# Twenty-four pairs of chunks of a value pass, multiplied by seven products of halves

## The chip, the cores and the metric

The kernel runs on one core of a Trainium2 chip. The metric is the device time of one execution in microseconds, lower is better. The kernel before was timed three times: 1837.2, 1838.18 and 1838.45 us, median 1838.18. The engines are named as in the profile: PE is TensorE, PEld its weight loads, DVE is VectorE, ACT is ScalarE, POOL is GpSimd, SP is the engine whose queue issues the loads.

## The reference

A two-layer decoder trunk over 256 tokens of width 1024. Each layer has a token mixer (mLSTM in layer 0, RG-LRU in layer 1) beside a memory cross-attention, a layer norm, a mixture of 16384 experts of one hidden unit each, and a second layer norm. What matters here is the expert step, which picks 128 experts for every token (8 heads of 16):

```python
u = u_tab[eid]
act = jax.nn.gelu(jnp.einsum('nhkd,nd->nhk', u, xb))
coef = (gw * act)
return jnp.einsum('nhk,nhkd->nd', coef, v_tab[eid])
...
x = layer_norm(DN_ALPHA * x + y, ln2_g[i], ln2_b[i])
```

Everything is float32.

## The kernel before

The kernel doesn't gather the experts. It computes the activations of all 16384 experts for all 256 tokens, multiplies them by a weight that is zero for an expert that wasn't picked, and multiplies the result with the whole value table. So each layer has two long passes over tables of 64 MB: the u pass, which makes activations, and **the value pass**, which the change is about.

The value pass goes over 128 chunks of 128 experts, `for i in range(P)` from L1104 in `peer_layer`. Chunk i has a coefficient tile of 128 experts x 256 tokens (a block of `wglo` for i < 64, of `wghi` from there on) and a value tile of 128 experts x 1024 columns, loaded from HBM into `raw`. The output y is 256 x 1024, held in four PSUM banks of 128 tokens x 512 columns over the whole pass.

**Three products for one.** The products run on values rounded to a shorter form (fp32r). Each operand is split into a rounded part H and a remainder L, and `mm3` (L165 to L169) issues H x H, H x L and L x H. A chunk has 2 token halves x 2 column halves x 3 = 12 products of 128x128 by 128x512.

**Preparing a chunk.** `pump` (L77) splits a value tile: ACT casts `raw` to `wH` (L97), and DVE subtracts to get `wL` (L112); `pool_cols` is 0 in this pass, so POOL takes no part of it. Then it issues the next load on SP's queue (`load`, L117). `coef` (L1083) does the same for the coefficients through `split_to` (L221): ACT casts to `cH` (L222), DVE subtracts to get `cL` (L223).

**What sets the order.** The program is scheduled by hand: each engine executes its instructions in the order in which they are written. Iteration i first calls `self.next`, which splits the value tile of chunk i + 2, then `coef(i + 2)`, then issues the products of chunk i. `wH`/`wL` and `cH`/`cL` have three buffers each (`HL_BUFS`), `raw` has five; a load is issued while fewer than five raw tiles are in flight (`n_flight`), and a raw tile is let go when it has been split. So a cast to `wH` for chunk i + 2 must wait until PE is done with chunk i - 1.

**Beside the pass.** In layer 0 the loads for the next layer's cross-attention are put between the value chunks by `plan` (L1182 to L1190): four tiles of `memT` (split by ACT and POOL) and four of `wkv` (split by ACT and DVE into `kH`, `kL`). When i + 2 reaches `N0` = 64 the memory of `wglo` is given to them (L1108); in layer 1 it is given to three extra value tiles (`eH`, `eL`) for the pass's end. The last chunks of the pass (`kept`) are multiplied bank by bank, so that the layer norm can begin on one bank while PE is at the next. `norm` (L254) first adds each bank onto x, scaled by `ALPHA` (L272).

Of the kernel before, what the change touches and what calls it, by code (L numbers as in the profile page):

```python
# [7 lines left out]
F32 = mybir.dt.float32  # L8
F32R = mybir.dt.float32r
# [4 lines left out]
ALU = mybir.AluOpType  # L14
# [4 lines left out]
P = 128  # L19
D = 1024  # L20
T = 256
DT = 8
ALPHA = 4.0 ** 0.25
EPS = 1e-5
GSCALE = 32768.0
N0 = 64
# [7 lines left out]
EXTRA = 3  # L34
MIX_COLS = 0
GAP = 56
CAND = [(0, 1, 16, 0), (1, 1, 8, 16), (2, 1, 5, 24), (3, 1, 4, 29), (4, 1, 3, 33), (5, 3, 2, 36), (8, 8, 1, 42)]
NCAND = 50
ROWS = [(16, 16), (24, 8), (29, 5), (33, 4), (36, 3), (38, 2), (40, 2), (42, 2)]
# [5 lines left out]
class Trunk:  # L45
    def __init__(self, ctx, tc, A, out):
        self.ctx, self.tc, self.nc, self.A, self.out = ctx, tc, tc.nc, A, out
        pool = lambda name, bufs=1, **k: ctx.enter_context(tc.tile_pool(name=name, bufs=bufs, **k))
        self.const = pool("const")
        self.raw = pool("raw", RAW_BUFS)  # L50
        self.hl = pool("hl", HL_BUFS)
        self.small = pool("small", 2)
        self.ps = pool("ps", 8, space=PSUM)
        self.items = []
        self.flip = False
        self.sides = []
        self.n_load = self.n_split = self.n_got = self.n_flight = 0
        self.kept = {}
        self.loaded, self.split = {}, {}

    def bank(self):
# [15 lines left out]
    def pump(self, upto):  # L77
        nc = self.nc
        upto = min(upto, len(self.items))
        while self.n_split < upto:  # L80
            i = self.n_split
            self.load(i + 1)
            ap, n, dest, keep, cuts = self.items[i]
            r = self.loaded.pop(i)
            self.n_split += 1
            if keep is not None:
                self.kept[keep] = r
                continue
            if type(dest) is int:
                h, l = self.extra[dest]  # L90
            elif dest is None:
                h = self.hl.tile([P, D], F32R, name="wH")[:, :n]
                l = self.hl.tile([P, D], F32R, name="wL")[:, :n]
            else:
                h, l = dest()
            for c in cuts:
                (nc.vector.tensor_copy if self.cast_dve else nc.scalar.copy)(h[:, c], r[:, c])  # L97
            k = n if getattr(dest, "pool", False) else min(n, self.pool_cols)
            if len(cuts) > 1:
                for c in cuts:  # L100
                    e = (nc.vector, nc.gpsimd)[c.start > 0]
                    e.tensor_sub(l[:, c], r[:, c], h[:, c].bitcast(F32))
                k = n
            elif k and self.chained:
                nc.vector.tensor_sub(l[:, k:], r[:, k:], h[:, k:].bitcast(F32))  # L105
                k += 2
                nc.gpsimd.tensor_sub(l[:, :k], r[:, :k], h[:, :k].bitcast(F32))  # L107
                k = n
            elif k:
                nc.gpsimd.tensor_sub(l[:, :k], r[:, :k], h[:, :k].bitcast(F32))  # L110
            if k < n:
                nc.vector.tensor_sub(l[:, k:], r[:, k:], h[:, k:].bitcast(F32))  # L112
            self.split[i] = (h, l)
            self.n_flight -= getattr(dest, "stage", None) is None
            self.load(len(self.items))

    def load(self, upto):  # L117
# [135 lines left out]

    def norm(self, y, last, early, fill=False):  # L254
        nc, x = self.nc, self.x
        fine = early or last
        while "b" not in self.kept:
            self.pump(self.n_split + 1)
        g, b = self.kept["g"], self.kept["b"]
# [4 lines left out]
        Q = 256  # L264

        def add(tt, k):
            if fine and tt and k:
                q0, n = 1 + k, 1
            else:
                q0, n = 2 * k, 2  # L270
            xs = x[:, tt, q0 * Q:(q0 + n) * Q]
            nc.vector.scalar_tensor_tensor(xs, xs, ALPHA, y[tt][k][:, :n * Q], op0=ALU.mult, op1=ALU.add)  # L272
            return tt, q0, n

        def half(tt, q0, n):
# [71 lines left out]
        else:  # L347
            yield
            part = add(1, 0)
# [3 lines left out]
        if early:  # L353
            yield
            part = add(1, 0)
# [611 lines left out]
    def peer_layer(self, layer):  # L967
        nc, tc, A = self.nc, self.tc, self.A
        with ExitStack() as ctx:
# [4 lines left out]
            lo = right.enter_context(tc.tile_pool(name=f"lo{layer}", bufs=1, side="right")).tile([P, N0, T], F32,  # L974
                                                                                               name="wglo")
# [104 lines left out]
            self.pool_cols, self.chained = 0, False  # L1080
            kept = HL_BUFS + (EXTRA if layer else 0)

            def coef(i):  # L1083
                src = lo[:, i, :] if i < N0 else hi[:, i - N0, :]
                pool, z = (ends, i - P + kept) if layer and i >= P - kept else (cp, "")
                cH = pool.tile([P, T], F32R, name=f"cH{z}")
                cL = pool.tile([P, T], F32R, name=f"cL{z}")
                self.split_to(cH, cL, src)
                return cH, cL
            cs = [coef(0), coef(1)]  # L1090
            g = self.u_step()
            gl = cp.tile([P, T], F32, name="gl", bufs=1)
            nc.scalar.activation(gl, g, AF.Gelu)
            nc.vector.tensor_mul(hi[:, nj - 1, :], hi[:, nj - 1, :], gl)
            y = [[self.bank() for _ in range(2)] for _ in range(2)]
            late = []

            def products(tt, c0, n, part):
                t = slice(tt * P, (tt + 1) * P)
                k, o = divmod(c0, 512)  # L1100
                for i_, (h, l), (cH, cL) in part:
                    self.mm3(y[tt][k][:, o:o + n], cH[:, t], cL[:, t], h[:, c0:c0 + n], l[:, c0:c0 + n],
                             i_ == 0, i_ == P - 1)
            for i in range(P):  # L1104
                if i + 2 > P - 1:
                    self.pool_cols = 512
                late.append((i, self.next(min(HL_BUFS, P - i)), cs.pop(0)))
                if i + 2 == N0:  # L1108
                    right.close()
                    if layer == 0:  # L1110
                        kv = self.later.enter_context(tc.tile_pool(name="kv1", bufs=1, side="right"))
                        m = right.enter_context(tc.tile_pool(name="mem1", bufs=1, side="right"))
                        self.mem_dest(kv, m)
                        m.tile([P, 80], F32, name="gap")
                        self.kvw = [(m.tile([P, D], F32R, name=f"kH{c}"), m.tile([P, D], F32R, name=f"kL{c}"))
                                    for c in range(4)]
                    else:
                        ends = right.enter_context(tc.tile_pool(name="ends", bufs=1, side="right"))
                        self.extra = [(ends.tile([P, D], F32R, name=f"eH{e}"), ends.tile([P, D], F32R, name=f"eL{e}"))
                                      for e in range(EXTRA)]  # L1120
                if i + 2 < P:
                    cs.append(coef(i + 2))
                if i + 1 > P - kept:
                    continue
                for tt in range(2):
                    for k in range(2):
                        products(tt, 512 * k, 512, late)
                late = []
            self.pool_cols = MIX_COLS
            if layer:  # L1130
# [17 lines left out]
    def plan(self):  # L1148
# [24 lines left out]
        def tail(layer):  # L1173
            for i, dt in enumerate((6, 7, 0, 1, 2, 3, 4, 5)):
                self.add(A["w_out"][layer, dt], D, i - 2 if 0 <= i - 2 < EXTRA else None)
            norm("ln1", layer)
            for g in range(2):
                for dt in range(DT):
                    self.add(A["w_q"][layer, g, dt], D)
            for i in range(P):  # L1180
                self.add(A["u"][layer, i], D)
            for i in range(P):  # L1182
                e = i - P + HL_BUFS + EXTRA
                self.add(A["v"][layer, i], D, e if layer and 0 <= e < EXTRA else None)
                k = (i - N0 - 4) // 6
                if layer == 0 and i > N0 and (i - N0 - 4) % 6 == 0 and 0 <= k < 8:
# [106 lines left out]
```

## Time and profile before

The profiled execution of the kernel before:

| what | us |
|---|---|
| its own time | 1838.14 |
| its span | 1836.4 |
| layer 0's value pass, first product to last (start) | 581.5 to 929.5 |
| PE busy in the span | 1806.4 |
| PEld busy | 1665.8 |
| DVE busy | 1297.5 |
| ACT busy | 941.4 |
| POOL busy | 433.1 |

The time lies 1.7 us above the span: the span runs from the first to the last instruction of the profile. A row of the groups view has the line, engine and operation, the tiles written and read, the shape, the count, then the busy time, the mean duration of one in ns, and the idle time of the engine ahead of it with what ended it. A row of the timeline has start and duration in us; what stands in brackets is the engine's idle time before it and what ended that. Line numbers in these rows are those of the kernel before.

### The profile page before, as it was taken

The numbers are of one execution on the slowest core, as the hardware profiler recorded it, in microseconds if no ns is written. First come the engines' busy times: TensorE is split into PE (matmuls) and PEld (weight loads), VectorE is DVE, ScalarE is ACT, GpSimd is POOL, SyncE is SP. The second block draws the span as 40 slices with busy tenths as digits, with TensorE's granted clock in tenths as the row PEclk, the third lists the DMA queues.
The fourth block names the chain that finished last, engine by engine and source line by source line (L and its number), as shares of the span: only waits on it lengthen the run. The fifth ranks groups of instructions, "written<-read, shape, count | busy, mean of one in ns | idle before, by whom it ended". The sixth has DMA issues, their size and how long they took to land.

```text
span 1836.4 us, 33231 instructions
## 1 busy us (share of the span) xinstructions
PE 1806.4 (98%) x12756; PEld 1665.8 (91%) x12756; DVE 1297.5 (71%) x2652; ACT 941.4 (51%) x1608; POOL 433.1 (24%) x324
## 2 busy tenths in 40 slices
PE   8999999999999999999999899999999999999998
PEld 8999999999999888888898699999999988888886
DVE  5674669599998555666568648795999965555556
ACT  6554555455545444555547355554555455555443
POOL 2005772333331000000011368335333300000000
PEclk9999999999999999999999899999999999999999
DMA  6656566655555666667654355666555566666664
GB/s 235 208 158 187 173 186 194 195 172 162 161 161 164 192 196 193 195 217 226 209 186 133 118 174 183 192 196 187 161 162 161 162 182 194 193 192 193 194 194 137
DMA packets 95265, 334.21 MB, mean 182 GB/s; under 512 B 10621, under 2 KB 13697, under 8 KB 94849
## 3 DMA queue, kind: packets, MB, share of 16 engines
q1 hardware_dynamic: 93464, 328.93, 58.6%
q10 hardware_dynamic: 1640, 3.15, 0.5%
q8 instruction: 100, 1.64, 0.4%
q14 instruction: 61, 0.49, 0.1%
HBM read 330.98 MB, written 1.05 MB: 181 GB/s over the span
## 4 chain that ended last, share of the span: by engine, by line
PE 73%; issue 15%; POOL 7%; DVE 3%; ACT 2%; DMA 0%; POOLq 0%; DVEq 0%; SPq 0%; ACTq 0%
PE bank L167 23%; PE bank L169 23%; PE bank L168 23%; POOL wL L107 7%; PE bank L226 2%; ACT wH L97 1%; DVE wL L112 0%; PE bank L319 0%; DVE aa L765 0%; DVE xc L731 0%; POOL wL L110 0%; DVE st L278 0%; DVE x L272 0%; ACT pr L451 0%; DMA cp<-in_rg_par_dram 0%
## 5 line engine op out<-in xcount | busy, mean ns | idle before, releaser
L97 ACT CAST wH<-raw 128x1024 fp32r<-128x1024 f32 (+2 forms) x605 | 628.6, 1040 | 772.5 <-PE bank L169 323.3
L112 DVE TENSOR_TENSOR wL<-raw,wH 128x1024 fp32r<-128x1024 f32 (+3 forms) x410 | 464.1, 1134 | 452.1 <-ACT wH L97 451.4
L167 PE MATMUL bank<-xHL,wH 128*128 128x256 f32 x2536 | 717.5, 283 | 7.1 <-ACT wH L97 6.2
L169 PE MATMUL bank<-xHL,wL 128*128 128x256 f32 x2536 | 704.5, 278 | 2.2 <-DVE wL L112 2.2
L168 PE MATMUL bank<-xHL,wH 128*128 128x256 f32 x2536 | 704.6, 278 | 0.0
L167 PEld LDWEIGHTS bank<-xHL,wH 128*128 128x128 f32 x2536 | 479.5, 189 | 7.9 <-ACT wH L97 6.2
L169 PEld LDWEIGHTS bank<-xHL,wL 128*128 128x128 f32 x2536 | 479.3, 189 | 3.1 <-DVE wL L112 2.8
L168 PEld LDWEIGHTS bank<-xHL,wH 128*128 128x128 f32 x2536 | 479.9, 189 | 0.3 <-DVE xHL L223 0.3
L168 PE MATMUL bank<-wL,cH 128*128 128x512 f32 x1015 | 394.3, 388 | 0.0
L169 PE MATMUL bank<-wH,cL 128*128 128x512 f32 x1015 | 394.3, 388 | 0.0
L167 PE MATMUL bank<-wH,cH 128*128 128x512 f32 x1015 | 394.3, 388 | 0.0
L110 POOL TENSOR_TENSOR wL<-raw,wH 128x1024 fp32r<-128x1024 f32 (+1 forms) x121 | 259.1, 2145 | 212.8 <-ACT wH L97 212.2
L169 PEld LDWEIGHTS bank<-wH,cL 128*128 128x128 f32 x1015 | 190.5, 188 | 39.7
L167 PEld LDWEIGHTS bank<-wH,cH 128*128 128x128 f32 x1015 | 190.5, 188 | 39.4
L168 PEld LDWEIGHTS bank<-wL,cH 128*128 128x128 f32 x1015 | 190.5, 188 | 39.0
L107 POOL TENSOR_TENSOR wL<-raw,wH 128x386 fp32r<-128x386 f32 x126 | 129.6, 1029 | 280.0 <-DVE wL L105 280.0
L308 POOL TENSOR_TENSOR x<-x,raw 128x256 f32<-128x256 f32 x6 | 4.8, 805 | 556.7 <-ACT x L305 556.7
L929 DVE TENSOR_TENSOR oh<-iota,i12T 128x1024 f16<-128x1024 f16 x128 | 130.2, 1017 | 0.0
L105 DVE TENSOR_TENSOR wL<-raw,wH 128x640 fp32r<-128x640 f32 x126 | 103.9, 825 | 7.7
L932 DVE TENSOR_TENSOR oh<-oh,gT 128x1024 f16<-128x1024 f16 x128 | 90.0, 703 | 4.4
L1062 PE MATMUL bank<-oh 128*128 128x128 f16 x1024 | 80.9, 220 | 1.1 <-DVE oh L932 1.1
L1062 PEld LDWEIGHTS <-oh 128*128 128x128 f16 x1024 | 58.8, 97 | 6.0 <-DVE oh L932 1.5
(273 smaller groups left out, 1527.7 us busy)
## 6 DMA issues: line engine op xcount, KB each, us to landing
raw<-in_u_dram SPq DMA_DIRECT2D x256, 512.0 KB, 3.7
raw<-in_v_dram SPq DMA_DIRECT2D x256, 512.0 KB, 4.3
raw<-in_w_q_dram SPq DMA_DIRECT2D x32, 512.0 KB, 3.8
raw<-in_w_out_dram SPq DMA_DIRECT2D x16, 512.0 KB, 4.5
raw<-in_w0qx_dram SPq DMA_DIRECT2D x8, 512.0 KB, 4.8
raw<-in_wkv_dram SPq DMA_DIRECT2D x8, 512.0 KB, 4.7
raw<-in_w1x_dram SPq DMA_DIRECT2D x8, 512.0 KB, 4.5
raw<-in_w0v_dram SPq DMA_DIRECT2D x8, 384.0 KB, 6.1
```

What stands on the lines that cost most here:

```text
L97: (nc.vector.tensor_copy if self.cast_dve else nc.scalar.copy)(h[:, c], r[:, c])
L105: nc.vector.tensor_sub(l[:, k:], r[:, k:], h[:, k:].bitcast(F32))
L107: nc.gpsimd.tensor_sub(l[:, :k], r[:, :k], h[:, :k].bitcast(F32))
L110: nc.gpsimd.tensor_sub(l[:, :k], r[:, :k], h[:, :k].bitcast(F32))
L112: nc.vector.tensor_sub(l[:, k:], r[:, k:], h[:, k:].bitcast(F32))
L167: mm(out, sH, mH, start=start, stop=False, skip_group_check=True)
L168: mm(out, sH, mL, start=False, stop=False, skip_group_check=True)
L169: mm(out, sL, mH, start=False, stop=stop, skip_group_check=True)
L226: self.nc.tensor.matmul(out, lhsT, rhs, start=start, stop=stop, skip_group_check=True)
L929: nc.vector.tensor_tensor(flat(oh[:, 1:3]), self.iota2.unsqueeze(1).to_broadcast([P, 4, P, 2]), pairs(self.i12T[:, j]), op=ALU.is_equal)
L932: nc.vector.tensor_tensor(flat(oh[:, 0:2]), two.rearrange("p z (q e t) -> p z q e t", q=2, t=2), pairs(self.gT[:, j]), op=ALU.mult)
L1062: nc.tensor.matmul(wp[:, qs], oh[:, 2, q // 2, :, q % 2], oh[:, z, q // 2, :, q % 2], start=z == 0, stop=z == 1, skip_group_check=True)
```

## The change

In each value pass the chunks are seen in groups of eight, and in most groups (`PAIRS`: eleven in layer 0, thirteen in layer 1) the third and the fourth chunk, 8k + 2 and 8k + 3, are multiplied together as a 2 x 2 block product: two chunks by two halves of the tokens on one side, two chunks by two halves of the columns on the other. Strassen's scheme (in Winograd's form) needs seven block products in place of eight. Each is three products on PE as before.

The seven products are spread over the group. Chunk 8k + 2 has one (into the new bank `m1`), chunk 8k + 3 has two (into `y[0][0]` and `y[0][1]`). Three (`m5`, `m7`, `m6`) follow behind the products of chunk 8k + 7, and the last (`y[1][0]`) behind those of chunk 8k + 8. The four m banks are kept over the whole pass, and are combined once, behind the last pair, by `onto` and the additions on `q`; that scales x by `ALPHA` there, so `norm` doesn't.

The operands of the scheme are sums. DVE makes them in float32 in blocks of `wglo` or `wghi` whose chunks are done (`sums32`); then ACT casts them and DVE subtracts, as for any operand, into the tile `xHL`, which isn't used otherwise in this pass (`th`, `tl` for the value sums, `sh`, `sl` for the coefficient sums). `paired(i)` issues these steps at set places of the group, behind `coef(i + 2)` and ahead of the products of chunk i. The raw tiles of the pair are held until the step at 8k + 4 has read them. Of the first chunk of a pair only the first 512 columns are split.

The memory of `wglo` is given away later (`CLOSE` = 76 in place of 64), and layer 0's extra loads stand after every fifth chunk from 80 in place of every sixth from 68.

```diff
+PAIRS = [[1, 2, 3, 4, 5, 6, 7, 8, 9, 11, 12], list(range(1, 14))]
+CLOSE = 76
...
+            z = self.twin.get(i)
+            if z is not None:
+                self.pair[z] = r
+                n = min(n, 512 * (z + 1))
+                cuts = [slice(0, n)]
...
-            self.n_flight -= getattr(dest, "stage", None) is None
+            self.n_flight -= getattr(dest, "stage", None) is None and z is None
...
+            th, tl = self.xHL[:, 0:3, :], self.xHL[:, 3:6, :]
+            sh, sl = (self.xHL[:, f, :].rearrange("p (f t) -> p f t", f=4) for f in (6, 7))
...
+            def split_sums(k, f, n, s):
...
+                nc.vector.tensor_sub(tl[:, s:s + n], t, plain(th[:, s:s + n]))
+            def cast_sums(k, f, n, s):
...
+                nc.scalar.copy(th[:, s:s + n], t)
+            def paired(i):
+                k, j = divmod(i, 8)
+                if k - 1 in PAIRS[layer] and j == 0:
+                    cast_sums(k - 1, 3, 1, 0), split_sums(k - 1, 3, 1, 0)
+                if k in PAIRS[layer]:
+                    t, s = sums32(k)
+                    if j in (2, 4):
+                        (a0, a1), (b0, b1) = [[r[:, :512], r[:, 512:]] for r in self.pair]
+                    if j == 0:
+                        (ta, ua), (tb, ub) = part(i + 2), part(i + 3)
+                        nc.vector.tensor_sub(s[:, 1], ta, ua)
+                        nc.vector.tensor_sub(s[:, 2], ub, s[:, 1])
+                        nc.vector.tensor_add(s[:, 0], ua, ub)
+                        nc.scalar.copy(sh[:, 0:3], s[:, 0:3])
+                    elif j == 2:
+                        nc.vector.tensor_sub(t[0], a1, a0)
+                        nc.vector.tensor_sub(t[1], b1, a1)
+                        cast_sums(k, 0, 2, 0)
+                    elif j == 4:
+                        nc.vector.tensor_add(t[2], t[1], a0)
+                        nc.vector.tensor_sub(t[3], b0, t[2])
+                        cast_sums(k, 2, 1, 2)
+                        self.n_flight -= 2
+                        self.load(len(self.items))
+                    elif j == 5:
+                        split_sums(k, 0, 2, 0)
+                    elif j == 6:
+                        split_sums(k, 2, 1, 2)
...
             def coef(i):
...
+                if i in first:
+                    cH, cL = cp.tile([P, T], F32R, name="cH"), cp.tile([P, T], F32R, name="cL")
+                    self.split_to(cH[:, :P], cL[:, :P], src[:, :P])
+                    return cH, cL
+                if i - 1 in first:
...
+                    nc.vector.tensor_sub(s[:, 3], src[:, :P], s[:, 2])
+                    nc.scalar.copy(cH[:, :P], src[:, :P])
+                    nc.scalar.copy(cH[:, P:], s[:, 3])
+                    nc.scalar.copy(sh[:, 3], src[:, P:])
+                    nc.vector.tensor_sub(cL[:, :P], src[:, :P], plain(cH[:, :P]))
+                    nc.vector.tensor_sub(cL[:, P:], s[:, 3], plain(cH[:, P:]))
+                    nc.vector.tensor_sub(sl[:, 0:3], s[:, 0:3], plain(sh[:, 0:3]))
+                    nc.vector.tensor_sub(sl[:, 3], src[:, P:], plain(sh[:, 3]))
+                    return cH, cL
...
+            m1, m5, m7, m6 = [self.bank() for _ in range(4)]
...
                 if i + 2 < P:
                     cs.append(coef(i + 2))
+                paired(i)
...
+                if i in first or i - 1 in first:
+                    (_, (h, l), (cH, cL)), = late
+                    if i in first:
+                        mixed(m1, h[:, :512], l[:, :512], (cH[:, :P], cL[:, :P]), first[i])
+                    else:
+                        mixed(y[0][0], h[:, :512], l[:, :512], (cH[:, :P], cL[:, :P]))
+                        mixed(y[0][1], h[:, 512:], l[:, 512:], (cH[:, P:], cL[:, P:]))
+                else:
+                    for tt in range(2):
+                        for k in range(2):
+                            products(tt, 512 * k, 512, late)
+                if i % 8 == 7 and i // 8 in PAIRS[layer]:
+                    for f, b in enumerate((m5, m7, m6)):
+                        mixed(b, th[:, f], tl[:, f], (sh[:, f], sl[:, f]), i // 8)
+                if i % 8 == 0 and i // 8 - 1 in PAIRS[layer]:
+                    mixed(y[1][0], th[:, 0], tl[:, 0], (sh[:, 3], sl[:, 3]))
```

More of the change, by code (lines that the diff above doesn't have):

```diff
@@ L58, in __init__ @@
         self.kept = {}
+        self.twin, self.pair = {}, [None, None]
         self.loaded, self.split = {}, {}
@@ L111, in pump @@
             if k < n:
-                nc.vector.tensor_sub(l[:, k:], r[:, k:], h[:, k:].bitcast(F32))
+                nc.vector.tensor_sub(l[:, k:n], r[:, k:n], h[:, k:n].bitcast(F32))
             self.split[i] = (h, l)
-            self.n_flight -= getattr(dest, "stage", None) is None
+            self.n_flight -= getattr(dest, "stage", None) is None and z is None
             self.load(len(self.items))
@@ L255, in norm @@
         nc, x = self.nc, self.x
+        alpha = 1.0 if last or fill else ALPHA
         fine = early or last
@@ L271, in add @@
             xs = x[:, tt, q0 * Q:(q0 + n) * Q]
-            nc.vector.scalar_tensor_tensor(xs, xs, ALPHA, y[tt][k][:, :n * Q], op0=ALU.mult, op1=ALU.add)
+            nc.vector.scalar_tensor_tensor(xs, xs, alpha, y[tt][k][:, :n * Q], op0=ALU.mult, op1=ALU.add)
             return tt, q0, n
@@ L1081, in peer_layer @@
             kept = HL_BUFS + (EXTRA if layer else 0)
-            def coef(i):
-                src = lo[:, i, :] if i < N0 else hi[:, i - N0, :]
+            block = lambda i: lo[:, i, :] if i < N0 else hi[:, i - N0, :]
+            part = lambda i: [block(i)[:, :P], block(i)[:, P:]]
+            first = {8 * k + 2: k for k in PAIRS[layer]}
+            done = 8 * PAIRS[layer][-1] + 8
+            gl = cp.tile([P, T], F32, name="gl", bufs=1)
+            th, tl = self.xHL[:, 0:3, :], self.xHL[:, 3:6, :]
@@ new lines, in peer_layer, with sums32 @@
+            sh, sl = (self.xHL[:, f, :].rearrange("p (f t) -> p f t", f=4) for f in (6, 7))
+            plain = lambda a: a.bitcast(F32)
+            def sums32(k):
+                old = hi if k > 8 else lo
+                flat = lambda b: old[:, b:b + 2, :].rearrange("p a b -> p (a b)")
+                return [flat(b) for b in (0, 2, 4, 6)], flat(8).rearrange("p (f t) -> p f t", f=4)
+            def split_sums(k, f, n, s):
+                old = hi if k > 8 else lo
+                t = old[:, 2 * f:2 * (f + n), :].rearrange("p (f a) b -> p f (a b)", f=n)
+                nc.vector.tensor_sub(tl[:, s:s + n], t, plain(th[:, s:s + n]))
@@ new lines, in cast_sums, with onto @@
+            def cast_sums(k, f, n, s):
+                old = hi if k > 8 else lo
+                t = old[:, 2 * f:2 * (f + n), :].rearrange("p (f a) b -> p f (a b)", f=n)
+                nc.scalar.copy(th[:, s:s + n], t)
[27 more added lines that the diff above has]
+                        split_sums(k, 2, 1, 2)
+                q = hi[:, 0:2, :].rearrange("p a b -> p (a b)")
+                def onto(t, h, src, scale=ALPHA):
+                    xs = self.x[:, t, 512 * h:512 * h + 512]
+                    nc.vector.scalar_tensor_tensor(xs, xs, scale, src, op0=ALU.mult, op1=ALU.add)
+                n = i - done
+                if n == 1:
+                    nc.scalar.copy(q, m1)
+                    onto(0, 0, m1)
+                elif n == 2:
+                    nc.vector.tensor_add(q, q, m6)
+                elif n == 3:
+                    onto(0, 1, q)
+                elif n == 4:
+                    onto(0, 1, m5, 1.0)
+                elif n == 5:
+                    nc.vector.tensor_add(q, q, m7)
+                elif n == 6:
+                    onto(1, 0, q)
+                elif n == 7:
+                    onto(1, 1, q)
+                elif n == 8:
+                    onto(1, 1, m5, 1.0)
@@ new lines, in mixed @@
+            def mixed(out, mh, ml, stat, k=None):
+                self.mm3(out, *stat, mh, ml, k == PAIRS[layer][0], k == PAIRS[layer][-1])
+            def coef(i):
+                src = block(i)
+                if i in first:
[3 more added lines that the diff above has]
+                if i - 1 in first:
+                    cH, cL = cp.tile([P, T], F32R, name="cH"), cp.tile([P, T], F32R, name="cL")
+                    _, s = sums32(i // 8)
+                    nc.vector.tensor_sub(s[:, 3], src[:, :P], s[:, 2])
[7 more added lines that the diff above has]
+                    return cH, cL
@@ L1091, in peer_layer @@
             g = self.u_step()
-            gl = cp.tile([P, T], F32, name="gl", bufs=1)
             nc.scalar.activation(gl, g, AF.Gelu)
@@ L1107, in peer_layer @@
                 late.append((i, self.next(min(HL_BUFS, P - i)), cs.pop(0)))
-                if i + 2 == N0:
+                if i + 2 == CLOSE:
                     right.close()
@@ L1122, in peer_layer @@
                     cs.append(coef(i + 2))
+                paired(i)
                 if i + 1 > P - kept:
                     continue
-                for tt in range(2):
-                    for k in range(2):
-                        products(tt, 512 * k, 512, late)
+                if i in first or i - 1 in first:
[14 more added lines that the diff above has]
+                    mixed(y[1][0], th[:, 0], tl[:, 0], (sh[:, 3], sl[:, 3]))
                 late = []
@@ L1183, in tail @@
                 e = i - P + HL_BUFS + EXTRA
+                if i % 8 in (2, 3) and i // 8 in PAIRS[layer]:
+                    self.twin[len(self.items)] = i % 8 - 2
                 self.add(A["v"][layer, i], D, e if layer and 0 <= e < EXTRA else None)
-                k = (i - N0 - 4) // 6
-                if layer == 0 and i > N0 and (i - N0 - 4) % 6 == 0 and 0 <= k < 8:
+                k, j = divmod(i - 80, 5)
+                if layer == 0 and j == 0 and 0 <= k < 8:
                     if k < 4:
```

## The prediction, made before the result was known

> **What bounds the kernel now.** I read the page first: the span, the engines' shares and the chain that ended last.
>
> ```profile
> span 1836.4 us, 33231 instructions
> PE 1806.4 (98%) x12756; PEld 1665.8 (91%) x12756; DVE 1297.5 (71%) x2652; ACT 941.4 (51%) x1608; POOL 433.1 (24%) x324
> ...
> PE 73%; issue 15%; POOL 7%; DVE 3%; ACT 2%; DMA 0%; POOLq 0%; DVEq 0%; SPq 0%; ACTq 0%
> ```
>
> TensorE is busy nearly all the time and holds most of the chain. A busy PE need not be PE at its peak, so I then read the stretch that the change touches: the stages view in the middle of layer 0's value pass, and a few rows of the timeline there.
>
> ```profile
> 690.00:740.00 50.00, 50.00 (x223) 41.39 (x222) 28.55 (x38) 24.94 (x37) 0.00 (x0) 1.00 0.66 193
> ```
>
> ```profile
> 690.12 0.39 PE L169 MATMUL bank<-wH,cL 128*128 128x512 f32 x1
> ...
> 690.35 0.39 PE L167 MATMUL bank<-wH,cH 128*128 128x512 f32 x1
> ...
> 690.55 1.05 ACT L97 CAST wH<-raw 128x1024 fp32r<-128x1024 f32 x1 [1.36 <-PE bank L169]
> ...
> 691.50 0.40 ACT L222 CAST cH<-wglo 128x256 fp32r<-128x256 f32 x1
> 691.63 1.23 DVE L112 TENSOR_TENSOR wL<-raw,wH 128x1024 fp32r<-128x1024 f32 x1 [1.16 <-ACT wH L97]
> ...
> 692.78 0.42 DVE L223 TENSOR_TENSOR cL<-wglo,cH 128x256 fp32r<-128x256 f32 x1
> ...
> 693.07 0.39 PE L167 MATMUL bank<-wH,cH 128*128 128x512 f32 x1
> 693.27 1.05 ACT L97 CAST wH<-raw 128x1024 fp32r<-128x1024 f32 x1 [1.36 <-PE bank L169]
> ```
>
> The stages columns are PE, PEld, DVE, ACT, POOL, then the granted clock (1.00). PE has no gap; DVE is busy 28.55 of 50 us, ACT 24.94. One chunk takes 693.07 - 690.35 = 2.72 us for 12 products, so 0.227 us a product. The loop runs at PE's pace: each cast of wH waits for the last product of the chunk that frees its buffer, and starts 690.55 - 690.35 = 0.20 us after that chunk's slot has ended.
>
> From that slot end to a complete cL (692.78 + 0.42 = 693.20) the preparation takes 2.85 us. It is for the chunk that PE reaches two chunks later, 5.44 us after the slot end. So **the look-ahead has 2.6 us to spare**, and it is the width of two chunks on PE that provides it.
>
> **What goes.** A pair costs 7 x 3 = 21 products in place of 24. The built order of PE has 13384 rows in place of 13456: 72 fewer, which is 24 pairs x 3. So the change does what it says, and at 0.227 us that is -0.68 us a pair, -16.3 us in all, if nothing waits.
>
> **What comes, and on which engine.** Nearly all of it goes into the queues of DVE and ACT.
>
> ```profile
> L97 ACT CAST wH<-raw 128x1024 fp32r<-128x1024 f32 x571 | 600.7, 1053 | 750.0 <-PE bank L169 315.6 <-POOL wL L107 187.5 <-PE bank L168 117.6
> L112 DVE TENSOR_TENSOR wL<-raw,wH 128x1024 fp32r<-128x1024 f32 x324 | 396.1, 1225 | 327.9 <-ACT wH L97 327.4
> L112 DVE TENSOR_TENSOR wL<-raw,wH 128x512 fp32r<-128x512 f32 x56 | 38.8, 693 | 108.6 <-ACT wH L97 108.6
> L223 DVE TENSOR_TENSOR cL<-wglo,cH 128x256 fp32r<-128x256 f32 x128 | 53.3, 418 | 0.3
> L298 DVE SCALAR_TENSOR_TENSOR x<-x,rs,raw 128x512 f32<-128x512 f32 x9 | 7.1, 785 | 0.3
> ```
>
> Per pair, DVE gets four sums of 512 columns (4 x 0.69), their splits (1.23 + 2 x 0.69), and ten or so narrow operations of 128 to 384 columns. For 128 columns no clean row stands; the line through 0.42 (256) and 0.69 (512) gives an estimate of 0.28. Half the split of the first chunk goes (-0.54). That is about 6.8 us by durations. The eight ordinary preparations of a group cost 8 x (1.23 + 0.42) = 13.2, so DVE has some 20 us of work in a group of 21.1 us; the overlap that the timeline shows (a next operation may start 0.08 us before the last one ends: 691.63 + 1.23 against 692.78) brings some 30 operations to about 17.6. Tight, but DVE is **not** the bound by its sum. ACT gets about 2.8 us on 11.6. The order of the queues decides.
>
> **The order.** Call the chunks of a group 0 to 7; 2 and 3 are the pair. On PE they are now short: chunk 2 has 3 products (0.68 us), chunk 3 has 6 (1.36 us); the nine others stand behind chunk 7, and three behind the next chunk 0. So the look-ahead that covered 5.44 us covers 2.04 us there. In that very place the built order has, on ACT: cast of wH for chunk 4, its cH, **the 1024-wide cast of two sums (th)**, then the cast of wH for chunk 5. On DVE: wL and cL of chunk 4, the two sums, then wL and cL of chunk 5. The new cast waits for the second sum, and behind it on ACT stands chunk 5's cast, for which DVE and then PE wait. ACT has nothing that it could take first.
>
> Timed from the slot end of chunk 1 on PE, with the rows above:
>
> - 0.20: cast for chunk 4 (its buffer was chunk 1's), to 1.25. DVE's wL starts at 1.28 (hand-over 0.03, as at 691.63); cL starts 1.15 later, at 2.43, and ends at 2.85.
> - 2.77: first sum; 3.38: second sum, to 4.07. I take the 0.69 of the other 512-wide subtraction in SBUF; the bounds are 0.42 (the 256-wide row) and 0.79 (L298).
> - 4.10: cast of the sums; the next cast starts 0.95 later (as 690.55 to 691.50), at 5.05: this is chunk 5's wH, to 6.10.
> - 6.13: wL of chunk 5; 7.28: its cL, to 7.70.
>
> PE needs that cL for the third product of chunk 5. Unhindered, it gets there 3 + 6 + 12 + 2 = 23 products after the slot end: 5.21 us. How PE restarts is shown at the kernel's end:
>
> ```profile
> 1826.19 0.42 DVE L272 SCALAR_TENSOR_TENSOR x<-x,bank 128x256 f32<-128x256 f32 x1 [0.65 <-PE bank L169]
> ...
> 1826.67 0.39 PE L167 MATMUL bank<-eH,cH 128*128 128x256 f32 x1 [0.51 <-DVE x L272]
> ...
> 1826.89 0.28 PE L168 MATMUL bank<-eL,cH 128*128 128x256 f32 x1
> ```
>
> Product and weight load start 0.06 us after DVE's end, and the next product 0.22 later where 0.12 is usual, so a restart costs about 0.16. PE goes on at 7.87: **2.66 us late**. Chunk 4's own wait (its cL at 2.85 against a need at 2.49) lies inside that. The rest of the group has chunk 6 and then 21 products in a row, so its preparations are in time again, but PE has no idle time in which to make the 2.66 good. Per pair: +2.66 - 0.68 = +1.98. For 24 pairs: **+47.5 us**. It doesn't depend on the neighbours: the wait arises inside one group.
>
> Smaller terms. One of layer 0's groups (the twelfth) has a wkv chunk among its items right behind its chunk 4; its cast and split stand between th and chunk 5:
>
> ```profile
> L112 DVE TENSOR_TENSOR kL<-raw,kH 128x1024 fp32r<-128x1024 f32 x4 | 4.9, 1219 | 0.0
> L97 ACT CAST kH<-raw 128x1024 fp32r<-128x1024 f32 x4 | 4.2, 1048 | 0.0
> ```
>
> That is 1.2 us more on DVE ahead of chunk 5's wL, and chunk 6, pushed back as well, waits about as long again: +2.4 us, an estimate. Before, the spare 2.6 us hid it. The additions onto x (eight of 512 columns behind the last pair, one a chunk) lie in DVE's idle 43%; the products that are put off need their sums' splits by chunk 7, over 10 us later, and have them. SP's queue and the loads: the pair's two raw buffers are held until chunk 4's step, so the load for the next group's chunk 0 starts only when chunk 5's wL is done. Chunk 1's slot ends 27 products (6.12 us) into the group, so that is at 6.12 + 6.13 + 1.23 = 13.5; ACT gets to its cast at about 17.7, behind chunk 7's.
>
> ```profile
> raw<-in_v_dram SPq DMA_DIRECT2D x256, 512.0 KB, 4.3
> ```
>
> It lands at 17.8, and PE wants that chunk only at 23.7: nothing. Added to the profiled execution (1838.14 us, which is the median of the runs to 0.04): 1838.1 + 47.5 + 2.4 = **1888 us**.
>
> **Rivals.** (a) *The queues keep up and PE's count decides.* This speaks for it: PE is at 98%, DVE's sum still fits. Then 1838.1 - 16.3 = 1821.8, faster. It decides at the chain above: if chunk 5's cL is ready by 5.2 us after chunk 1's slot, not 7.7, all of it is gained, and below 5.9 some. For that the sums and their cast, 2.3 us, must cost the queues nothing. Even without the ACT cast in the way, DVE would have chunk 5's cL at about 5.7. 8%. [...]
>
> (b) *PE's clock drops in the new gaps.* The granted clock of two stretches of before (same columns as above):
>
> ```profile
> 136.00:139.00 3.00, 2.36 (x20) 2.15 (x18) 2.92 (x7) 0.59 (x1) 3.00 (x2) 1.00 0.37 22
> 139.00:142.00 3.00, 0.66 (x2) 0.29 (x2) 1.74 (x5) 0.59 (x2) 3.00 (x17) 0.83 0.72 201
> ```
>
> With 0.6 us idle in 3 it stays at 1.00; with 2.3 idle it shows 0.83. The gaps here sum to 2.66 in about 5 us, the longest some 1.2, in between the two. If the clock halved for 3.4 us a group, 1.7 us would be added to each: 1888 + 41 = 1929. 5%. [...]
>
> (c) *The loads come late.* That chunk 0's split stands on DVE ahead of the last sum's, which PE wants 23.3 us into the group; cast, split, cL and that last split are 3.2 us, so the load may take 20.1 - 13.5 = 6.6 us. At 8.5 us it would cost some 1.9 a pair: 1888 + 46 = 1934. Against it: 4.3 us in the row above. 4%.
>
> (d) *Only about half of the wait is seen,* because the steps of the chain overlap more than their rows show: 1836 to 1868. 5%.
>
> **How the numbers follow.** 78% for the forecast. With the sums at 0.42 the chain is 0.5 shorter (-13 us); with 0.79 and some hand-overs at 0.1, up to 0.6 longer (+14). So 1874 to 1902 for the forecast alone; 1868 to 1906 with the edges of (b) and (d), which leaves out (a), (c) and most of (b) and (d), under 2 in 10. A measurement can tell 0.2% (3.7 us) from no change. Faster is (a): 0.08; the low edge of (d) gives 0.02 for the same; slower 0.90.
>
> **What would show it.** In the profile after: PE busy share down, three waits of PE a group at chunks 4 and 5 on the casts and wL/cL, 2.5 to 2.8 us together; the cast into xHL with idle before it, put down to a sum on DVE; chunk 5's wH cast right behind it; a granted clock of 1.00; group spacing 23.7 us in place of 21.76. A spacing of 21.1 makes me wrong by (a); a clock under 1.00 means (b); waits for raw mean (c).

## The result, and the profile after

The changed kernel takes 1897.72 us (median of 4 runs, 1896.11 to 1898.81), the kernel before 1837.69 (4 runs beside it). The ratio is 1.0327, 95% interval 1.0315 to 1.0339: **60 us slower**, where 1888 was forecast and 1868 to 1906 was the range.

The page of the changed kernel, with the same lines as were read of before (its line numbers are 8 or more higher: L97 is L105 here, L112 L120, L222 L230, L167 to L169 are L175 to L177):

```profile
span 1897.0 us, 33668 instructions
PE 1823.2 (96%) x12684; PEld 1651.9 (87%) x12684; DVE 1443.8 (76%) x3004; ACT 993.9 (52%) x1754; POOL 432.4 (23%) x324
...
PE 62%; issue 18%; DVE 7%; POOL 7%; ACT 5%; DMA 0%; POOLq 0%; ACTq 0%; DVEq 0%; SPq 0%
```

PE has 72 instructions fewer and is nevertheless busy for longer, since a product behind a wait is shown longer (0.49 or 0.50 us in the rows below, in place of 0.39) and the clock is halved for a while in three groups, as shown further down. What tells is the chain: DVE and ACT now hold 12% of it, before 5%. Who held PE up in layer 1's value pass is in the waits of PE from 1480 us on:

```profile
PE bank L175 <- ACT cH L230: 13.1, 13, 1.0
PE bank L176 <- DVE wL L120: 8.9, 27, 0.5
```

Thirteen pairs, thirteen waits of 1.0 us for ACT, and two short ones a pair for DVE. Before, PE didn't wait once in the middle of that pass. The stages view of two groups of layer 0 has the engines' shares (PE, PEld, DVE, ACT, POOL, then the granted clock):

```profile
700.00:748.00 48.00, 44.69 (x189) 34.72 (x188) 36.18 (x61) 26.02 (x44) 0.00 (x0) 1.00 0.53 176
```

DVE is busy for 36.18 of 48 us and ACT for 26.02: neither is full while PE waits. Here is one group's timeline on ACT and DVE, from the cast for chunk 4 on (chunks of a group counted from 0, the pair is 2 and 3):

```profile
728.88 1.05 ACT L105 CAST wH<-raw 128x1024 fp32r<-128x1024 f32 x1 [0.40 <-ACT xHL L1186]
729.84 0.40 ACT L230 CAST cH<-wglo 128x256 fp32r<-128x256 f32 x1
732.82 1.05 ACT L1117 CAST xHL<-wglo 128x1024 fp32r<-128x1024 f32 x1 [2.58 <-DVE wglo L1135]
733.78 1.04 ACT L105 CAST wH<-raw 128x1024 fp32r<-128x1024 f32 x1
734.72 0.40 ACT L230 CAST cH<-wglo 128x256 fp32r<-128x256 f32 x1
```

```profile
729.97 1.23 DVE L120 TENSOR_TENSOR wL<-raw,wH 128x1024 fp32r<-128x1024 f32 x1 [0.69 <-ACT wH L105]
731.11 0.42 DVE L231 TENSOR_TENSOR cL<-wglo,cH 128x256 fp32r<-128x256 f32 x1
731.45 0.69 DVE L1134 TENSOR_TENSOR wglo<-raw 128x512 f32<-128x512 f32 x1
732.05 0.69 DVE L1135 TENSOR_TENSOR wglo<-raw 128x512 f32<-128x512 f32 x1
734.85 1.23 DVE L120 TENSOR_TENSOR wL<-raw,wH 128x1024 fp32r<-128x1024 f32 x1 [2.11 <-ACT wH L105]
735.99 0.42 DVE L231 TENSOR_TENSOR cL<-wglo,cH 128x256 fp32r<-128x256 f32 x1
```

And the same stretch on PE:

```profile
730.68 0.39 PE L175 MATMUL bank<-wH,cH 128*128 128x512 f32 x1
731.25 0.50 PE L176 MATMUL bank<-wL,cH 128*128 128x512 f32 x1 [0.18 <-DVE wL L120]
...
735.18 0.49 PE L175 MATMUL bank<-wH,cH 128*128 128x512 f32 x1 [1.03 <-ACT cH L230]
736.13 0.49 PE L176 MATMUL bank<-wL,cH 128*128 128x512 f32 x1 [0.46 <-DVE wL L120]
736.46 0.50 PE L177 MATMUL bank<-wH,cL 128*128 128x512 f32 x1
736.80 0.40 PE L175 MATMUL bank<-wH,cH 128*128 128x512 f32 x1
```

ACT is ready at 730.24 and stands idle for 2.58 us, because the cast of the sums (L1117) is next in its queue and waits for the second sum (L1135, done at 732.74). DVE, for its part, has nothing to do for 2.11 us after that sum, because chunk 5's cast stands behind L1117 on ACT. Two engines wait for each other in turn, both idle for a while, and PE waits for both. The product at 736.80 is the 25th after chunk 1's slot end (730.68 less 9 products, 728.64): 8.16 us where 24 products take 5.44, so PE is 2.72 us late.

The stretches of the two passes, from the first product to the next stage's (in layer 1 to the last addition onto x):

| | layer 0's pass | layer 1's pass | groups' spacing |
|---|---|---|---|
| before | 348.2 | 349.6 | 21.76 |
| after | 382.1 | 378.8 | 23.92 |
| more | 33.9 (11 pairs) | 29.2 (13 pairs) | 2.16 |

(The spacing is that of the regular groups: those with a pair, without layer 0's groups 1, 11 and 12.) Layer 1 pays 2.24 us a pair, first and last group with it. Layer 0 pays 9 us more than 11 x 2.24 = 24.6. Of these, 1.5 us are group 1's: it takes 25.46 us in place of 23.92, and the granted clock (the third figure from the right) is 0.50 for a stretch right behind its waits:

```profile
612.51:615.92 3.41, 1.99 (x8) 1.01 (x7) 2.27 (x3) 2.67 (x5) 0.00 (x0) 1.00 0.17 67
615.92:619.34 3.42, 3.42 (x10) 2.67 (x9) 2.48 (x5) 1.87 (x3) 0.00 (x0) 0.50 0.79 242
```

The others are in groups 11 and 12, the ones among the extra loads. The granted clock around group 11:

```profile
846.00:849.00 3.00, 2.38 (x11) 1.65 (x10) 3.00 (x7) 0.41 (x1) 0.00 (x0) 1.00 0.57 175
849.00:852.00 3.00, 0.89 (x3) 0.29 (x1) 0.94 (x2) 2.50 (x3) 0.00 (x0) 0.91 0.00 0
852.00:855.00 3.00, 2.54 (x6) 1.81 (x6) 3.00 (x4) 2.00 (x4) 0.00 (x0) 0.50 0.27 67
855.00:858.00 3.00, 3.00 (x8) 2.32 (x8) 1.99 (x4) 0.67 (x2) 0.00 (x0) 0.50 0.96 321
858.00:861.00 3.00, 3.00 (x14) 2.41 (x13) 1.97 (x2) 2.10 (x4) 1.10 (x1) 0.95 0.98 367
```

PE had been idle for 2.11 us there; then the clock is halved for over 6 us. The row from 855, at 0.50 with no idle time, counts 8 products; the next one, at 0.95, counts 14. Group 12 shows the same (0.53, 0.50 and 0.83 from 882 to 891 us). With 3 x (0.09 + 0.50 + 0.50 + 0.05) = 3.4 us of lost clock in group 11, 3.4 in group 12, less what falls on idle time, that is about 6 of the 9 us.

### The profile page after: what moved, and what is told of

Read it like the earlier page. It is cut to its first block, busy times and chain, and to the rows that moved or that the text cites. A ratio compares the mean times of both kernels' runs of the same rounds, so it can differ in the third digit from the quotient of the medians.

```text
span 1897.0 us, 33668 instructions
## 1 busy us (share of the span) xinstructions
PE 1823.2 (96%) x12684; PEld 1651.9 (87%) x12684; DVE 1443.8 (76%) x3004; ACT 993.9 (52%) x1754; POOL 432.4 (23%) x324
## 4 chain that ended last, share of the span: by engine, by line
PE 62%; issue 18%; DVE 7%; POOL 7%; ACT 5%; DMA 0%; POOLq 0%; ACTq 0%; DVEq 0%; SPq 0%
PE bank L176 20%; PE bank L177 20%; PE bank L175 20%; POOL wL L115 7%; ACT wH L105 3%; DVE wL L120 2%; PE bank L234 2%; DVE cL L231 1%; DVE wglo L1135 1%; DVE wglo L1134 1%; DVE xc L740 0%; DVE wghi L1135 0%; DVE wghi L1134 0%; PE bank L328 0%; DVE aa L774 0%
## 5 line engine op out<-in xcount | busy, mean ns | idle before, releaser
L105 ACT CAST wH<-raw 128x1024 fp32r<-128x1024 f32 (+3 forms) x605 | 616.8, 1021 | 579.1 <-POOL wL L115 187.5
L120 DVE TENSOR_TENSOR wL<-raw,wH 128x1024 fp32r<-128x1024 f32 (+3 forms) x410 | 451.4, 1104 | 360.8 <-ACT wH L105 359.9
L175 PE MATMUL bank<-xHL,wH 128*128 128x256 f32 x2536 | 717.0, 283 | 7.0 <-ACT wH L105 6.1
L177 PE MATMUL bank<-xHL,wL 128*128 128x256 f32 x2536 | 703.5, 277 | 2.2 <-DVE wL L120 2.2
L175 PEld LDWEIGHTS bank<-xHL,wH 128*128 128x128 f32 x2536 | 478.8, 189 | 7.5 <-ACT wH L105 6.1
L177 PEld LDWEIGHTS bank<-xHL,wL 128*128 128x128 f32 x2536 | 478.6, 189 | 3.0 <-DVE wL L120 2.8
L175 PE MATMUL bank<-wH,cH 128*128 128x512 f32 x895 | 353.9, 395 | 26.3 <-ACT cH L230 22.2
L176 PE MATMUL bank<-wL,cH 128*128 128x512 f32 x895 | 356.6, 398 | 17.0 <-DVE wL L120 17.0
L177 PE MATMUL bank<-wH,cL 128*128 128x512 f32 x895 | 356.6, 398 | 0.0
L176 PEld LDWEIGHTS bank<-wL,cH 128*128 128x128 f32 x895 | 169.7, 190 | 70.3 <-DVE wL L120 35.4
L175 PEld LDWEIGHTS bank<-wH,cH 128*128 128x128 f32 x895 | 169.7, 190 | 70.0 <-ACT cH L230 31.6
L177 PEld LDWEIGHTS bank<-wH,cL 128*128 128x128 f32 x895 | 169.6, 190 | 41.4 <-DVE cL L231 1.8
L1117 ACT CAST xHL<-wglo 128x512 fp32r<-128x512 f32 (+1 forms) x48 | 36.6, 763 | 75.4 <-DVE wglo L1135 41.2
```

The lines of the kernel that those rows point to most:

```text
L120: nc.vector.tensor_sub(l[:, k:n], r[:, k:n], h[:, k:n].bitcast(F32))
L175: mm(out, sH, mH, start=start, stop=False, skip_group_check=True)
L176: mm(out, sH, mL, start=False, stop=False, skip_group_check=True)
L177: mm(out, sL, mH, start=False, stop=stop, skip_group_check=True)
```

## The experiments

Theories: **queue** (the cast waits on ACT for a sum, and chunk 5's cast stands behind it; the cover by PE's products has shrunk), **capacity** (DVE and ACT have too much to do in a group) and **clock** (the halved clock is the main cost).

### The cast of the sums, moved

```diff
                     elif j == 2:
                         nc.vector.tensor_sub(t[0], a1, a0)
                         nc.vector.tensor_sub(t[1], b1, a1)
-                        cast_sums(k, 0, 2, 0)
                     elif j == 4:
+                        cast_sums(k, 0, 2, 0)
                         nc.vector.tensor_add(t[2], t[1], a0)
```

> The cast of the two value sums moves on ScalarE from behind chunk 4's preparation to behind chunk 6's (step 8k + 4); sums, splits and products stay. Queue theory (the cast waits for a sum on VectorE and holds up chunk 5's cast behind it): chunk 5's cL is then complete about 5.6 us after chunk 1's slot end in place of 7.8, when it is wanted at 5.6 to 5.8; only chunk 4's own wait is left, about 0.56 us a pair against the 0.68 saved: 1834 to 1840 us, ScalarE's idle time ahead of the cast gone. Capacity theory (VectorE and ScalarE have too much to do in a group): the same work is left, about 1897. Clock theory (the lower clock costs most): only what the two slow groups cost comes back, about 1890.

1842.93 us (8 runs), 1.003 of before, interval 1.0019 to 1.0040. So 55 of the 60 us go with one line moved by two steps, all the work staying. Its timeline:

```profile
716.35 1.05 ACT L105 CAST wH<-raw 128x1024 fp32r<-128x1024 f32 x1 [0.40 <-ACT xHL L1186]
717.31 0.40 ACT L230 CAST cH<-wglo 128x256 fp32r<-128x256 f32 x1
...
717.62 1.04 ACT L105 CAST wH<-raw 128x1024 fp32r<-128x1024 f32 x1
...
721.25 0.42 DVE L231 TENSOR_TENSOR cL<-wglo,cH 128x256 fp32r<-128x256 f32 x1
```

ACT goes from chunk 4's cH straight to chunk 5's cast (717.62), and chunk 5's cL is complete at 721.67, 5.56 us after chunk 1's slot end at 716.11. The groups' spacing is 21.79 us, as before the change within 0.03. The capacity theory falls. The time is 3 to 9 us above the expected. A regular group loses 0.71 us to chunk 4's wait (21.79 less the 21.08 of 93 products) where 0.56 was expected, some 4 us for 24 pairs; and groups 11 and 12 have four waits of 0.63 to 1.00 us on wL, where a regular group has one of 0.18.

### The same cast in its old place, waiting for nothing

```diff
-                        cast_sums(k, 0, 2, 0)
+                        nc.scalar.copy(th[:, 0:2], self.x.rearrange("p a b -> p (a b)")[:, 0:1024].rearrange("p (f b) -> p f b", f=2))
```

> The cast stays where it is and as wide, but reads the residual x in place of the two sums, so it waits for no sum (the products m5 and m7 thus use other numbers). Queue theory: it is the wait and not the 1.05 us of work that counts; chunk 5's cast starts about 2.5 us after chunk 1's slot end, its cL is held by VectorE alone (5.6), and the time is as with the cast moved, 1834 to 1841. Theory that the cast's own 1.05 us on ScalarE is the cost: about 1897 less little, over 1890. Capacity theory: 1897.

1842.21 us (9 runs), 1.0024 (1.0014 to 1.0034): as with the cast moved. (The split that follows subtracts what was cast, so the L half holds the rest of the sum.) The cast takes the same 1.04 us at the same place of the queue, but starts at once:

```profile
720.00 0.40 ACT L230 CAST cH<-wglo 128x256 fp32r<-128x256 f32 x1
...
720.30 1.04 ACT L1136 CAST xHL<-x 128x1024 fp32r<-128x1024 f32 x1
721.25 1.05 ACT L105 CAST wH<-raw 128x1024 fp32r<-128x1024 f32 x1
```

So it is the wait, and not the work, that cost 55 us, with the halved clock that came with it: in this run as in the one before, both passes are at 1.00 throughout.

### The put-off products, moved

```diff
-                if i % 8 == 0 and i // 8 - 1 in PAIRS[layer]:
+                if i % 8 == 1 and i // 8 - 1 in PAIRS[layer]:
                     mixed(y[1][0], th[:, 0], tl[:, 0], (sh[:, 3], sl[:, 3]))
...
                     elif j == 5:
                         split_sums(k, 0, 2, 0)
+                        ub = part(8 * k + 3)[1]
+                        nc.scalar.copy(sh[:, 3], ub)
+                        nc.vector.tensor_sub(sl[:, 3], ub, plain(sh[:, 3]))
```

(and the same two operations taken out of `coef`)

> The three put-off products of a pair go behind the next group's chunk 1 in place of its chunk 0 (the cast and split of their coefficient operand move to step 8k + 5); the cast of the sums stays where it was. Queue theory: 0.68 us more of PE work lie between chunk 1's slot end and chunk 4, so each pair's wait shrinks from 2.72 to about 2.04: -16 us, 1881; if the two slow groups' gaps fall from 2.1 to 1.4 us and the clock holds there, 1874. Capacity theory: the order of PE's products changes nothing, 1897.

1894.58 us (4 runs), 1.0310 (1.0293 to 1.0327): only 3 us less than the changed kernel, not 16. The queue theory's mechanism holds, its sum doesn't. In layer 0's regular groups the spacing, from one group's first sum to the next one's, is 23.16 to 23.26 us where the clock holds, 0.7 less than 23.92, as expected; but two groups have 24.86. Here is one group whose clock holds and the next one, with the same gaps:

```profile
686.47 0.49 PE L175 MATMUL bank<-wH,cH 128*128 128x512 f32 x1 [0.95 <-ACT cH L230]
687.42 0.49 PE L176 MATMUL bank<-wL,cH 128*128 128x512 f32 x1 [0.46 <-DVE wL L120]
```

```profile
709.72 0.49 PE L175 MATMUL bank<-wH,cH 128*128 128x512 f32 x1 [0.95 <-ACT cH L230]
710.67 0.51 PE L176 MATMUL bank<-wL,cH 128*128 128x512 f32 x1 [0.46 <-DVE wL L120]
```

After the first the clock stays at 1.00; after the second it is halved, for 3.4 us (products come 0.43 us apart from 711.4 to 714.4). Both have 1.41 us of gaps. What differs is where the gaps lie. The traces record when the granted clock changes. In the changed kernel's the 13 times from one change to the next are whole multiples of 3.413 us (6.83, 23.89 and 6.83 us around its groups 11 and 12), and so are the 7 in the kernel before. A window here means 3.413 us counted on from such a change. The two groups cut into such windows, the one with the gaps and the one behind it for each:

```profile
683.94:687.36 3.42, 2.07 (x8) 1.15 (x7) 1.28 (x3) 3.24 (x5) 0.00 (x0) 1.00 0.34 139
687.36:690.77 3.41, 3.35 (x14) 2.70 (x15) 3.11 (x6) 1.27 (x4) 0.00 (x0) 1.00 0.68 171
707.84:711.25 3.41, 2.00 (x8) 1.04 (x7) 1.86 (x3) 3.08 (x5) 0.00 (x0) 1.00 0.25 103
711.25:714.67 3.42, 3.42 (x9) 2.63 (x9) 2.48 (x5) 1.61 (x3) 0.00 (x0) 0.50 0.74 204
```

In the first group 1.35 us of the gaps fall into one window (3.42 less PE's 2.07) and the rest into the next. In the second all 1.41 us fall into one, and the window behind it is halved. In the two passes of the changed kernel's profile and of the one before, some 430 windows are at full clock. The three with 1.42, 1.98 and 2.01 us of PE idle were each followed by a halved one; none with 1.39 us or less was. So in these two profiles the idle time within one window told the halved ones from the others. It doesn't tell them everywhere: between the changed kernel's passes a window (1066.48 to 1069.90) had 1.71 us and the clock held, and so it did behind one with 1.45 us in the run with the cast issued twice, below. What decides there isn't shown. The changed kernel's 23.92 us are 7.01 windows, so the gaps of its regular groups lie at nearly the same place of a window each time. Their windows had at most 1.39 us idle and none was hit; group 1's had 1.42 and was.

The mean granted clock of the whole span is 0.987 in place of the changed kernel's 0.992. Of the 13.6 us by which the time exceeds the expected 1881, that would be some 9 us (0.013 x 1891.9 less 0.008 x 1897.0), an estimate from these figures; where the others went isn't shown.

### Nine pairs in layer 0

```diff
-PAIRS = [[1, 2, 3, 4, 5, 6, 7, 8, 9, 11, 12], list(range(1, 14))]
+PAIRS = [[1, 2, 3, 4, 5, 6, 7, 8, 9], list(range(1, 14))]
```

> Layer 0's groups 11 and 12 are multiplied as before, nine pairs there in place of eleven. Queue theory alone: 2 x 2.2 us come back, 1893. With the clock (granted 0.50 for some 6.6 us in each of the two, 3.3 us lost in each) and the wkv and memT steps in those groups: about 14 us come back, 1884, and no stretch of the value passes below a clock of 1.00.

1889.00 us (4 runs), 1.0275 (1.0258 to 1.0293), 8.7 us back. Layer 0's pass itself gives the 14 us back: 368.1 us in place of 382.1, that is 2.2 us for each of nine pairs more than before. Of the 14, 1.6 us are group 1's, whose clock holds here (23.86 us in place of 25.46). Of what went again, 1.7 us are in layer 1's pass and 2.5 between the two passes. Layer 1's pass had a clock of 1.00 throughout in the changed kernel; here one window is halved, behind one with 1.49 us idle:

```profile
1675.19:1678.61 3.42, 1.93 (x8) 1.27 (x8) 2.69 (x4) 2.26 (x4) 0.00 (x0) 1.00 0.19 26
1678.61:1682.02 3.41, 3.41 (x10) 2.65 (x9) 2.47 (x5) 2.43 (x4) 0.00 (x0) 0.50 0.82 252
```

So groups 11 and 12 cost about 12 us, not 4.4, and a clock loss can appear in a pass in which nothing was edited.

### Both moves

The two edits above together.

> Both moves: the cast of the two sums behind chunk 6's preparation, and the three put-off products behind the next group's chunk 1. Queue theory: chunk 4's cL is ready 2.9 us after chunk 1's slot end and wanted at 3.2, chunk 5's at 5.6 and wanted at 5.9, so nothing waits in the 22 regular groups: group spacing 21.1 to 21.3 us against 21.76, -10 to -15 us; groups 11 and 12 of layer 0 keep some 4 us of waits: 1827 to 1833 us, granted clock 1.00. Capacity theory (VectorE, 84% busy in the group, can't keep pace): 1838 or more. Clock theory: gaps under 0.5 us, no stretch below 1.00.

1829.81 us (5 runs), 0.9957 (0.9943 to 0.9970): **faster than before by 8 us**, 0.4%. The spacing of regular groups is 21.17 us. PE's waits in layer 1's pass, from 1470 us on:

```profile
PE bank L176 <- DVE wL L120: 0.6, 2, 0.4
```

### The sums moved as well

```diff
-                    elif j == 2:
+                    elif j == 3:
                         nc.vector.tensor_sub(t[0], a1, a0)
                         nc.vector.tensor_sub(t[1], b1, a1)
```

> As with both moves, and the two sums themselves go on VectorE from behind chunk 4's cL to behind chunk 5's (step 8k + 3). Queue theory: they were covered already, so the regular groups stay at 21.1 to 21.3 us; in groups 11 and 12 they no longer stand ahead of a delayed split: 1825 to 1832 us. If VectorE's order still cost something in the regular groups, this would be clearly faster than with both moves alone, by over 5 us.

1828.48 us (5 runs), 0.9952 (0.9938 to 0.9966). No more than the scatter of the runs apart from both moves alone: where the sums stand on DVE costs nothing in the regular groups.

### The extra loads where no pair is

```diff
-                k, j = divmod(i - 80, 5)
-                if layer == 0 and j == 0 and 0 <= k < 8:
+                spots = (80, 82, 84, 86, 106, 110, 114, 118)
+                if layer == 0 and i in spots:
+                    k = spots.index(i)
```

> As the one with the sums late, and layer 0's eight extra loads are put where no pair is (behind chunks 80 to 86, and 106 to 118). Queue theory: the waits of groups 11 and 12 go, 24 pairs at -0.5 us: 1823 to 1828 us. If the extra loads aren't the cause of those two groups' waits: as without the move, 1825 to 1832.

1826.08 us (5 runs), 0.9933 (0.9920 to 0.9947): 11.5 us under before, 72 under the changed kernel. Layer 0's pass is 343.2 us (346.3 without this move), so the place of the extra loads was the cause of the waits left in groups 11 and 12. In this stretch of it DVE is busy 42.34 of 50 us and PE waits for nothing:

```profile
690.00:740.00 50.00, 50.00 (x221) 41.26 (x220) 42.34 (x71) 31.50 (x53) 0.00 (x0) 1.00 0.54 179
```

It is the best version found. Of the 16.3 us that 72 products are worth it has 11.5; the groups are 0.09 us longer than 93 products, 2 us in all. Some 3 us are left: the first pair behind a stretch without pairs (at 609.7, 822.9 and 1503.5 us) waits for wL and loses 0.6 us each time, and about 1 us goes near the end of layer 1's pass, at 1802 us.

### The cast twice

```diff
                         cast_sums(k, 0, 2, 0)
+                        cast_sums(k, 0, 2, 0)
```

> The changed kernel with the cast of the two sums issued twice, one behind the other. Queue theory alone: 0.95 us more a pair, 23 us: 1921. Clock theory (a gap of about 2 us, as in groups 11 and 12, always halves the clock for some 3.4 to 6.6 us): 1.7 to 3.3 us a pair on top, 1960 to 2000.

1945.17 us (2 runs), 1.0586 (1.0567 to 1.0606): 47 us over the changed kernel. It lies between the two expectations. The second cast makes the spacing 24.99 us in place of 23.92 where the clock holds, 26 us for 24 pairs; where it doesn't, the spacing is 26.6. PE's longest gap in a regular group is 2.08 us, and the clock is below 1.00 after some of them and not after others. The mean granted clock of the span is 0.980 in place of 0.992, which would be some 24 us more of lost clock (0.020 x 1944.1 less 0.008 x 1897.0), an estimate.

```profile
700.00:725.00 25.00, 22.28 (x87) 17.12 (x87) 18.05 (x31) 14.03 (x23) 0.00 (x0) 0.93 0.50 164
725.00:750.00 25.00, 22.29 (x94) 17.30 (x93) 17.45 (x30) 12.60 (x21) 0.00 (x0) 1.00 0.47 158
```

So a gap of 2 us didn't halve the clock each time either. Where it lay in the windows counted here too: around 694 us the group's idle time falls into two windows, 1.45 and 1.08 us, and the clock holds; around 719 us 2.18 us fall into one, and the next is halved.

## Why the prediction was right, and where it was off

- *What goes.* 72 products, 0.227 us each: right, and seen in the version with the queues in order (21.17 us a group against 21.76, where 21.08 was the floor).
- *The chain.* Right step by step. From chunk 1's slot end: cast at 0.24 (0.20 forecast), second sum done at 4.10 (4.07), cast of the sums at 4.18 (4.10), chunk 5's wH at 5.14 (5.05), its cL done at 7.77 (7.70), PE late by 2.72 (2.66). The value chosen for the sums, 0.69, is what they took.
- *The wait as the cause, and the queue as its reason.* Shown: moving the cast, or letting it read something that is ready, takes 55 us away with the work left in place.
- *DVE is not the bound.* Right: in the regular groups of the last version PE waits for nothing with DVE busy 85%.
- *Per pair.* 1.98 forecast, 2.16 measured in the regular groups: 0.06 from the chain, 0.12 from a few products that come 0.23 or 0.24 apart.
- *The smaller terms* were mis-sized: "+2.4 us" for the twelfth group, nothing for the eleventh. Measured: some 8 us for both, beyond a regular group's 2.2 each. The `memT` item between the eleventh group's chunks pushes its preparation back as `wkv` does in the twelfth, and PE's gaps of about 2 us there halved the clock, which cost about 6 of the 8.
- *Rival (b)*, the clock, was given 5% and "1.7 us to each" group. It came, in three groups of 24, with 3 us each in groups 11 and 12 and 1.5 in group 1. The forecast's "a granted clock of 1.00" was wrong there. The 3.4 us that it took for the halved clock stand in the profile of before (0.50 from 1018.18 to 1021.59 us). In the changed kernel's passes the clock fell behind windows of 3.41 us with 1.42, 1.98 and 2.01 us idle and held behind those with up to 1.39: that is between the two stretches from which the prediction judged (0.6 and 2.3 us idle in 3), so these could not decide it. That the 21 regular groups escaped was luck: their spacing is 7.01 windows, and their windows had up to 1.39 us idle. Had all been hit, at some 1.6 us each, the time would be about 1931 us, an estimate, which is rival (b)'s 1929 and outside the range.
- *Rival (a)*, the gain, is what the last versions have. "Even without the ACT cast in the way, DVE would have chunk 5's cL at about 5.7": it was at 5.56, and the spacing fell to that of before, no lower; chunk 4's own wait took the rest until the three products were moved.
- *Rival (c)*, late loads: ACT waited for raw tiles now and then (0.46 us at 742 us), PE never.

## What to carry to other kernels

Taking products away from the bound engine also takes away the cover under which the other engines prepare what it needs next: check the look-ahead in time, not in chunks, at the place where the work was taken out. Look in each engine's queue for an instruction that waits for another engine and ask what stands behind it; a new cast belongs behind the urgent one, even if it is ready later. Reshuffling the put-off work so that it falls into the thin place gave back what the thin place cost.

## What the runs showed of the hardware

In the traces of the kernel before and of the changed one, PE's granted clock changed only at times a whole multiple of 3.413 us apart, 20 of 20. In the changed kernel's passes it fell to 0.50 for one window of 3.413 us behind one in which PE had been idle for 1.42 us, and for two behind 2.01 and 1.98 us. With the products moved, 0.95 + 0.46 us around a single product were enough (3.41 us at 0.50); where the same gaps lay in two windows, as at 684 us, the clock held at 1.00. A halved window cost about 1.6 us there (24.86 us a group in place of 23.25), on top of the 1.41 us of gaps ahead of it, so these waits cost over twice their length. And an edit that shifts the groups can change the clock in another pass: in the nine-pair version's second layer, which wasn't edited, it fell to 0.50 from 1678.61 to 1682.02 us, where the changed kernel has 1.00 throughout.
